# Norm weights as a scale per channel, tiles turned into shared PSUM banks, and small buffers for the gate weights

## The chip, the cores and the metric

The kernel runs on one NeuronCore of a Trainium2 chip. The metric is device time in microseconds (us) of one execution, the median of several. TensorE (PE) multiplies matrices and writes PSUM, ScalarE (ACT) evaluates functions with a scale, VectorE (DVE) does elementwise work, and SyncE (SP) issues nearly all DMA transfers between DRAM and SBUF. Each engine works its own instructions off in order and waits on semaphores for the others.

## What is computed

One layer of a hybrid block on 16 meta tokens and 512 tokens of width 1024, batch 1. Only its start matters here:

```python
h = jnp.concatenate([meta, x], axis=1)                  # 528 tokens x 1024
xn = rms_norm(h, norm_mix_g[l])                         # x / rms(x) * g, per token, g per channel
z = xn @ w_in[l]                                        # 1024 x 10752
u_rnn, u_gate, q, k, v, g_ret, ga, gb = jnp.split(z, IN_SPLITS, axis=-1)
xr = causal_dwconv(u_rnn, rnn_conv_w[l], rnn_conv_b[l])     # 4 taps over time, u_rnn is 1280 wide
hr = rg_lru(xr, rg_a_w[l], rg_a_b[l], rg_x_w[l], rg_x_b[l], lru_lambda[l])
```

Then come a retention branch of four heads, two gated projections, a residual, a second norm, a convolved feed-forward part and a last norm.

## The kernel before

Every product of f32 values runs on TensorE as three f16 products: each operand is split into a high f16 part (ACT writes it, a scaled copy) and a low f16 part (DVE: scaled operand minus the high part), and hi*hi, hi*lo and lo*hi are summed in PSUM. The helper `split` (L90 to L92) issues both instructions. Here tile names stand for `xh`, `xl`, the high and low parts of the normed input, stored with channels on partitions (8 groups k of 128 channels) and tokens along the free axis, and `wt`, the split weights.

The input is 4 tiles of 128 tokens (`xin`, two tiles to a buffer) and 16 meta tokens (`xmeta`, stored as 128 rows of 128 channels). Per tile, `rms_scale` takes the sum of squares (ACT L320), its root (ACT L322) and a reciprocal (DVE L324). `first_rows` (L403) multiplies the tile by the token's factor and by `gmix`, the norm's weights copied to all 128 partitions. `first_transpose` turns it with eight TensorE transposes into two PSUM banks, and `finish` splits each bank of 128 x 512 into `xh` and `xl`.

The recurrent branch has ten output chunks of 128 columns (n = 0 to 9). A product of one chunk has two halves of 267 token columns, each 24 f16 matmuls (8 groups k, 3 terms). The first halves of n = 0, 1, 2 need tiles 0 and 1 only and are issued early (`first_half`, L383 in the profile), between the transposes of tiles 2 and 3; their second halves follow in `conv_product`. After each product `conv_taps` (L538 on ACT, L540 on DVE) sums the four taps, and `rnn_gates` (n - 3) runs the gate products. `keep_warm` issues matmuls on zeros, so that TensorE has something to do while the input is loaded; they write the first bank of the PSUM tile that chunk 0's product later uses (`early[0]`).

PSUM has three `acc` tiles of two banks and two single banks. The order of instructions on PE, ACT and DVE is the order of the code (`manual_schedule`). Weights come in units: `unit_load` fetches one into one of two f32 buffers (`raw`), `steps` holds its splits, `tick` issues the next split, `get` issues what a product needs. Loads on SyncE's queue keep the order in which the code issues them (`load`, L93 to L102), except a few early ones that do not depend on it (the decay table `dec_meta`, L690, and two gathers `hs` of meta tokens with 1024 elements of 4 bytes each, L1068).

Of the kernel before, what the change touches and what calls it, by code (L numbers as in the profile page):

```python
# [14 lines left out]
P = 128  # L15
T = 528
# [34 lines left out]
def hybrid_block_kernel(ctx, tc, x, meta, norm_mix_g, w_in, conv_w, conv_b, rg_a_w, rg_a_b,  # L51
# [159 lines left out]

    def fast_steps(rv, bk, bc):
# [88 lines left out]
    gmix = wsp.tile([P, D], F32, name="gmix", tag="wt")  # L301
# [53 lines left out]
    xn_t = {}  # L355
# [43 lines left out]
    def first_rows(i, rs):  # L399
        xn_t[i] = pair("xn")  # L400
        for a in range(2):
            sl = slice(a * 512, (a + 1) * 512)
            nc.vector.scalar_tensor_tensor(xn_t[i][a], token_rows(i)[:, sl], rs, gmix[:, sl], op0=ALU.mult, op1=ALU.mult)  # L403

    def first_transpose(i, banks):
        xn = xn_t.pop(i)
        c0 = 3 + NM + P * i
        pvs = []
        for a in range(2):
            pv = banks[a].rearrange("p (b c) -> p b c", c=P)  # L410
            for k in range(4):
                nc.tensor.transpose(pv[:, k], xn[a][:, k * P:(k + 1) * P], ident)
            pvs.append(pv)

        def finish(*half):
            for a in half:
                sl = slice(4 * a, 4 * a + 4)
                split(xh[:, sl, c0:c0 + P], xl[:, sl, c0:c0 + P], pvs[a], S_XN)
        return finish
# [14 lines left out]
    keep_warm(18)  # L434
    pmeta = acc("pmeta")[:, 0]
    xm, gm = xmeta[:, 0:P], xmeta[0:8, P:2 * P]
    first_rows(0, rms_scale(token_rows(0), P, "n"))
    finish0 = first_transpose(0, ptr_banks())
    first_rows(1, rms_scale(token_rows(1), P, "n"))
    ssm = small.tile([P, 4], F32, name="ssm")  # L440
    nc.scalar.activation(xmeta[:, 2 * P:3 * P], xm, AF.Square, accum_out=ssm[:, 0:1])
    nc.tensor.matmul(pmeta[:, 0:P], pick[0:8, 0:P], gm, start=True, stop=True)
    nc.tensor.matmul(pmeta[:, 2 * P:2 * P + 1], same[:, 0:P], ssm[:, 0:1], start=True, stop=True)
    finish0(0)
    finish0(1)
    keep_warm(2)
    pt1 = acc("pt1")
    finish1 = first_transpose(1, [pt1[:, 0], pt1[:, 1]])
    nc.scalar.activation(ssm[:, 1:2], pmeta[:, 2 * P:2 * P + 1], AF.Sqrt, scale=1.0 / D, bias=eps_t)
    nc.vector.reciprocal(ssm[:, 2:3], ssm[:, 1:2])  # L450
    nc.vector.scalar_tensor_tensor(xm, xm, ssm[:, 2:3], pmeta[:, 0:P], op0=ALU.mult, op1=ALU.mult)
    keep_warm(5)
    nc.tensor.transpose(pmeta[:, P:2 * P], xm, ident)
    keep_warm(6)
# [3 lines left out]

    first_step()
# [4 lines left out]
    first_rows(2, rms_scale(token_rows(2), P, "n"))  # L464
    first_half(0)
    for i in range(2):
        first_step()
    finish2 = first_transpose(2, ptr_banks())
    rs3 = rms_scale(token_rows(3), P, "n")
    finish2(0, 1)  # L470
    first_rows(3, rs3)
    first_half(1)
    queue(unit_load(2))
    for i in range(4):
        first_step()
    finish3 = first_transpose(3, ptr_banks())
    first_half(2)
    finish3(0, 1)
# [34 lines left out]
    def load_gates(nm):  # L513
        src = {"a": rg_a_w, "x": rg_x_w}[nm]
        raw = wraw.tile([P, 2048], F32, name="raw")
        load(raw[:, :DR].rearrange("p (n j) -> p n j", n=NR), src.rearrange("n i j -> i n j"))
        gw[nm] = ([piece([P, 2, 512], F16, "gw") for _ in range(3)], raw)

    def split_gates(nm):
        wt, raw = gw[nm]  # L520
        for i, n in enumerate((512, 512, 256)):
            split(wt[i][:, 0, :n], wt[i][:, 1, :n], raw[:, 512 * i:512 * i + n], SW)
# [56 lines left out]
    load_gates("x")  # L579
    for n in range(NR):  # L580
# [109 lines left out]
    nc.sync.dma_start(dec_meta, decay_t[:, :, T:].rearrange("h p c -> p h c"))  # L690
# [713 lines left out]
```

## Time and profile before

| What | Value |
|---|---|
| median of 3 runs | 1076.57 us (1076.39 to 1077.71) |
| profiled execution, its own time | 1076.25 us |
| its span in the trace | 1074.5 us |
| PE busy | 1055.9 us, 98% of the span |
| DVE busy, ACT busy | 839.0 us (78%), 567.5 us (53%) |
| DMA | 112.00 MB, mean 104 GB/s |

The span is the time between the first and the last event in the trace; the execution's own time is 1.75 us longer than it. "PEclk" is the TensorE clock that was granted: the page shows it at nine tenths or more in all 40 slices. The page puts an engine's idle time down to what released it, so a row with "[1.69 <-DVE xn L403]" says that the engine had been idle 1.69 us and that the xn instruction of line 403 on DVE ended it. A row of several instructions ("x18") gives the time from the start of the first to the end of the last.

### The profile page before, as it was taken

The numbers are of one execution on the slowest core, as the hardware profiler recorded it, in microseconds if no ns is written. First come the engines' busy times: TensorE is split into PE (matmuls) and PEld (weight loads), VectorE is DVE, ScalarE is ACT, GpSimd is POOL, SyncE is SP. The second block draws the span as 40 slices with busy tenths as digits, with TensorE's granted clock in tenths as the row PEclk, the third lists the DMA queues.
The fourth block names the chain that finished last, engine by engine and source line by source line (L and its number), as shares of the span: only waits on it lengthen the run. The fifth ranks groups of instructions, "written<-read, shape, count | busy, mean of one in ns | idle before, by whom it ended". The sixth has DMA issues, their size and how long they took to land.

```text
span 1074.5 us, 20950 instructions
## 1 busy us (share of the span) xinstructions
PE 1055.9 (98%) x9037; PEld 855.1 (80%) x9037; DVE 839.0 (78%) x1219; ACT 567.5 (53%) x847; POOL 6.8 (1%) x20
## 2 busy tenths in 40 slices
PE   8999999999999999999999999999999999999997
PEld 5888888865684858888888885588888888888885
DVE  6875799998786969878697785578767777888875
ACT  6558954435564747566454453365444544454442
POOL 2000000000000000000000000000000000000000
PEclk9999999999999999999999999999999999999999
DMA  7432243431212212423333355143232323113322
GB/s 220 133 117 80 80 138 119 157 120 40 80 41 72 88 62 65 128 89 119 103 104 119 118 200 174 38 159 118 79 118 80 119 79 118 41 60 126 111 79 79
DMA packets 108027, 112.00 MB, mean 104 GB/s; under 512 B 5546, under 2 KB 99472, under 8 KB 107936
## 3 DMA queue, kind: packets, MB, share of 16 engines
q1 hardware_dynamic: 107504, 110.27, 31.4%
q8 instruction: 70, 1.15, 0.4%
q10 hardware_dynamic: 144, 0.26, 0.1%
q0 software_dynamic: 288, 0.14, 0.1%
q14 instruction: 21, 0.17, 0.0%
HBM read 108.57 MB, written 2.10 MB: 103 GB/s over the span
## 4 chain that ended last, share of the span: by engine, by line
PE 75%; DVE 14%; ACT 8%; issue 2%; DMA 1%; SPq 0%; ACTq 0%; DVEq 0%
PE ps L370 33%; PE P L1240 9%; PE pa L776 9%; PE ps L839 4%; PE pm L370 4%; PE ps L1112 4%; PE pe L776 4%; DVE wt L92 3%; PE ps L383 3%; PE pb L776 2%; ACT wt L91 2%; PE ps L861 1%; DVE rnn L575 1%; DVE raw L231 1%; ACT L627 1%
## 5 line engine op out<-in xcount | busy, mean ns | idle before, releaser
L370 PEld LDWEIGHTS <-wt 128*128 128x128 f16 x4224 | 410.5, 97 | 63.7 <-DVE t L667 1.4
L92 DVE SCALAR_TENSOR_TENSOR wt<-raw,wt 128x1024 f16<-128x1024 f32 (+2 forms) x270 | 296.6, 1111 | 71.5 <-ACT wt L91 69.5
L91 ACT ACTIVATE wt<-raw 128x1024 f16<-128x1024 f32 (+2 forms) x270 | 256.4, 965 | 161.1 <-PE ps L370 28.3
L776 PEld LDWEIGHTS <-wt 128*128 128x128 f16 x2016 | 195.0, 97 | 36.0 <-issue 8.8
L370 PE MATMUL ps<-x2h,wt 128*128 128x258 f16 x1440 | 218.8, 273 | 0.0
L370 PE MATMUL ps<-xh,wt 128*128 128x257 f16 (+2 forms) x1056 | 163.8, 275 | 1.1 <-DVE t L667 1.1
L370 PE MATMUL ps<-x2l,wt 128*128 128x258 f16 x720 | 137.7, 272 | 0.0
L1197 DVE SCALAR_TENSOR_TENSOR cv<-ps,vt,cv 128x512 f32<-128x512 f32 x96 | 71.9, 749 | 54.7 <-ACT cv L1195 53.4
L370 PE MATMUL ps<-xl,wt 128*128 128x257 f16 (+2 forms) x528 | 102.2, 275 | 0.0
L1240 PE MATMUL P<-wt,act 128*128 128x256 f16 x792 | 88.3, 273 | 0.0
L1240 PEld LDWEIGHTS <-act 128*128 128x128 f16 x792 | 77.5, 98 | 9.0
L839 PE MATMUL ps<-wt,xh 128*128 128x512 f16 x256 | 76.4, 379 | 1.2 <-DVE v L92 1.0
L776 PE MATMUL pa<-xs,wt 128*128 128x257 f16 x576 | 71.6, 273 | 4.8 <-ACT kept L781 4.5
L1195 ACT ACTIVATE cv<-ps,vt,vt 128x512 f32<-128x512 f32 x48 | 37.1, 773 | 56.8 <-PE ps L370 52.2
L370 PE MATMUL pm<-oa,wt 128*128 128x257 f16 x480 | 55.4, 274 | 0.0
L839 PEld LDWEIGHTS <-xh 128*128 128x128 f16 x256 | 24.8, 98 | 30.9 <-issue 2.9
L839 PE MATMUL ps<-wt,xl 128*128 128x512 f16 x128 | 48.5, 379 | 0.0
L776 PE MATMUL pa<-ob,wt 128*128 128x257 f16 x384 | 45.7, 274 | 0.6 <-ACT last L781 0.5
L1112 PE MATMUL ps<-wt,mx 128*128 128x512 f16 x192 | 44.3, 379 | 0.0
L231 DVE TENSOR_TENSOR raw<-raw 128x1024 f32<-128x1024 f32 x35 | 42.7, 1220 | 0.6
L1112 PEld LDWEIGHTS <-mx 128*128 128x128 f16 x192 | 17.6, 98 | 18.5
L861 PE MATMUL ps<-sc,v 128*128 128x257 f16 (+4 forms) x384 | 32.1, 236 | 0.0
(250 smaller groups left out, 1273.5 us busy)
## 6 DMA issues: line engine op xcount, KB each, us to landing
raw<-in_w_in SPq DMA_DIRECT2D x41, 1024.0 KB, 4.8
raw<-in_w_up SPq DMA_DIRECT2D x24, 1024.0 KB, 5.0
raw<-in_w_down SPq DMA_DIRECT2D x48, 256.0 KB, 3.4
raw<-in_w_branch_ret SPq DMA_DIRECT2D x16, 512.0 KB, 4.3
raw<-in_w_branch_rnn SPq DMA_DIRECT2D x8, 640.0 KB, 4.2
raw<-in_w_out SPq DMA_DIRECT2D x4, 1024.0 KB, 4.9
xin<-in_x SPq DMA_DIRECT2D x4, 512.0 KB, 4.9
h<-in_x SPq DMA_DIRECT2D x4, 512.0 KB, 4.3
```

Of the source, the lines that this page charges most:

```text
L91: nc.scalar.activation(hi, src, AF.Copy, scale=s)
L92: nc.vector.scalar_tensor_tensor(lo, src, s, hi, op0=ALU.mult, op1=ALU.subtract)
L231: nc.vector.tensor_tensor(pair, pair, rv[:, :, right].rearrange("p (h k) c -> p h k c", h=2), op=ALU.add)
L370: nc.tensor.matmul(ps[:, hf, :n], w(aw, k, col, P), src(ax, k, c0, n), start=k == 0 and (aw, ax) == (0, 0), stop=k == nk - 1 and aw == 1)
L383: mm = nc.tensor.matmul(ps[:, hf, :n], w(aw, k, col, P), src(ax, k, c0, n), start=k == 0 and (aw, ax) == (0, 0), stop=k == KD - 1 and aw == 1)
L776: nc.tensor.matmul(ps[:, :257], ws[k // 4](wf, aw, k % 4), src(xf_, ax, k), start=first and k == 0 and (aw, ax) == (0, 0), stop=k == last_ ...
L839: nc.tensor.matmul(pb, xf(ax, k, XF + j0, nb), w(aw, k % 4, 0, 512), start=i == 0, stop=i == 23)
L861: nc.tensor.matmul(ps[:, hf, s0 - lo_i:257], vt[b][:, va, d * P:(d + 1) * P], st[SCP[b][0]][:, sa, o:o + hi_i - s0], start=i == 0, stop=i ...
L1112: nc.tensor.matmul(ps[:, n], mx[k][:, a, c0:c0 + P], wo[k // 2](aw, k % 2, n * 512, 512), start=k == 0 and (a, aw) == (0, 0), stop=k == ks ...
L1195: nc.scalar.activation(vv_, ps[:, :, 2:258], AF.Identity, scale=vt2[:, 96 + ch:97 + ch], bias=b_ff[:, ch:ch + 1])
L1197: nc.vector.scalar_tensor_tensor(vv_, ps[:, :, j:j + 256], vt2[:, 48 * j + ch:48 * j + ch + 1], vv_, op0=ALU.mult, op1=ALU.add)
L1240: nc.tensor.matmul(pd[:, 256 * tt:256 * tt + 256], t[:, ax, c0 + tt * P:c0 + tt * P + P], w(wf, aw, i), start=q % 6 == 0 and tt == 0 and i ...
```

## The change

The weights of the first norm are no longer multiplied in before the transposes. They are brought to one column per channel group (`gs`, 128 x 8, by a small transpose of the 8 x 128 weights), and are the scale operand of the split: because a channel is a partition after the transpose, the scale differs from group to group, and each split of 128 x 512 becomes four of 128 x 128 (`high`, `low`). The buffer `gmix` and its load go.

For tiles 0 and 1 the token's factor goes into a diagonal matrix `dg` (identity times factor, L429), and TensorE turns and scales at once by multiplying the f32 tile with it (L452). For tiles 2 and 3 a `tensor_scalar` multiplies by the factor (L437), followed by the transposes as before (L450). Tile 1's second half, and tile 3, are turned into the second, still unused banks of `early[0]` and `early[1]`; tiles 2 and 3 are turned together, ahead of the third early product.

The first two weight chunks are one unit of 256 columns, fetched and split by columns in two pieces. The gate weights are loaded into six pieces of 128 x 512 and not into the two `raw` buffers, and are split at other places. `dec_meta` is loaded in order with the rest, and one `hs` gather then stands first on SyncE's queue, the second one behind the first two input tiles. The number of `keep_warm` matmuls changes from 18, 2, 5 and 6 to 11, 4 and 5.

```diff
-    for n in range(2):
-        u_ur.append((unit(8, P, [(0, 0, kmaj(w_in, 0, 8, o_ur + P * n, P))]), 0))
-    for i in range(1, 5):
+    for i in range(5):
         u = unit(8, 256, [(0, 0, kmaj(w_in, 0, 8, o_ur + 256 * i, 256))])
...
+    def column_unit():
...
+        def fetch(c):
+            load(rv[:, :, c * P:c * P + P], ap[:, :, c * P:c * P + P])
+        def step(i, c):
...
+                split(tv[0], tv[1], rv[:, 4 * i:4 * i + 4, c * P:c * P + P], SW)
+        queue([step(i, c) for c in range(2) for i in range(2)])
...
+    nc.scalar.dma_start(xmeta[0:8, P:2 * P], norm_mix_g.rearrange("(c f) -> c f", f=P))
     load(xin[0][:, 0], x2[0:P])
     load(xin[0][:, 1], x2[P:2 * P])
-    load(gmix, norm_mix_g.partition_broadcast(P))
     load(xmeta[:, 0:P], meta.rearrange("t (c f) -> (t c) f", f=P))
-    load(xmeta[0:8, P:2 * P], norm_mix_g.rearrange("(c f) -> c f", f=P))
-    queue(unit_load())
+    fetch = column_unit()
+    fetch(0)
     load(xin[1][:, 0], x2[2 * P:3 * P])
-    queue(unit_load())
+    fetch(1)
     load(xin[1][:, 1], x2[3 * P:4 * P])
+    fetch = column_unit()
+    fetch(0)
+    fetch(1)
...
+    def first_scale(i):
+        rs = rms_scale(token_rows(i), P, "n")
+        dg = piece([P, 512], F32, "dg")[:, 0:P]
+        nc.vector.tensor_scalar_mul(dg, ident, rs)
+        return dg
...
+        def turn(a):
             for k in range(4):
+                c = 512 * a + k * P
+                if dg is None:
+                    nc.tensor.transpose(pvs[a][:, k], xn[a][:, k * P:k * P + P], ident)
+                else:
+                    nc.tensor.matmul(pvs[a][:, k], token_rows(i)[:, c:c + P], dg, start=True, stop=True)
+        def high(a):
+            for k in range(4):
+                g = gs[:, 4 * a + k:4 * a + k + 1]
+                nc.scalar.activation(xh[:, 4 * a + k, c0:c0 + P], pvs[a][:, k], AF.Copy, scale=g)
+        def low(a):
+            for k in range(4):
+                g = gs[:, 4 * a + k:4 * a + k + 1]
+                nc.vector.scalar_tensor_tensor(xl[:, 4 * a + k, c0:c0 + P], pvs[a][:, k], g,
+                                               xh[:, 4 * a + k, c0:c0 + P], op0=ALU.mult, op1=ALU.subtract)
...
+    keep_warm(11)
...
+    dg0 = first_scale(0)
+    turn0, high0, low0 = first_transpose(0, ptr_banks(), dg=dg0)
+    nc.tensor.transpose(pmeta[:, 3 * P:3 * P + 8], gm, ident[0:8, 0:8])
+    nc.vector.tensor_scalar_mul(gs, pmeta[:, 3 * P:3 * P + 8], S_XN)
+    turn0(0)
+    turn0(1)
+    dg1 = first_scale(1)
+    pt1 = acc("pt1")
+    turn1, high1, low1 = first_transpose(1, [pt1[:, 0], early[0][:, 1]], dg=dg1)
+    high0(0)
+    nc.scalar.activation(xmeta[:, 2 * P:3 * P], xm, AF.Square, accum_out=ssm[:, 0:1])
+    high0(1)
...
+    turn1(0)
...
+    turn1(1)
+    nc.scalar.activation(ssm[:, 1:2], pmeta[:, 2 * P:2 * P + 1], AF.Sqrt, scale=1.0 / D, bias=eps_t)
+    low0(0)
+    low0(1)
+    nc.vector.reciprocal(ssm[:, 2:3], ssm[:, 1:2])
+    nc.vector.scalar_tensor_tensor(xm, xm, ssm[:, 2:3], pmeta[:, 0:P], op0=ALU.mult, op1=ALU.mult)
+    keep_warm(4)
+    nc.tensor.transpose(pmeta[:, P:2 * P], xm, ident)
+    keep_warm(5)
     first_step()
-    finish1(0)
+    high1(0)
     split(xh[:, :, 3:3 + NM], xl[:, :, 3:3 + NM], pmeta[:, P:2 * P].rearrange("p (t c) -> p c t", c=8), S_XN)
+    low1(0)
     first_step()
-    finish1(1)
...
+    high1(1)
+    low1(1)
     first_half(0)
...
+    xn2 = first_rows(2)
+    xn3 = first_rows(3)
     first_half(1)
+    turn2, high2, low2 = first_transpose(2, ptr_banks(), xn=xn2)
+    turn3, high3, low3 = first_transpose(3, [early[i][:, 1] for i in range(2)], xn=xn3)
...
     first_half(2)
...
+        raw = [piece([P, 512], F32, "graw") for _ in range(3)]
...
-            tick(2 if n in (6, 8) else 1)
+            tick(2 if n in (4, 6, 8) else 1)
```

On TensorE, where the last `keep_warm` matmul and the first f16 product meet (before: `ps_125` is the tile `early[0]`):

```order
L427 MATMUL ps_125<-warm_123 128x512
L383 LDWEIGHTS wt_213 [waits Activation_49]
L383 MATMUL ps_125<-xh_95,wt_213 128x267 [waits Activation_49]
L383 LDWEIGHTS wt_213
L383 MATMUL ps_125<-xl_96,wt_213 128x267 [waits DVE_49]
```

The same place in the changed kernel, where `early[0]` is `ps_126`, L452 turns tile 1's second half, L510 turns the meta rows, L473 is `keep_warm` and L406 the product:

```order
L452 MATMUL ps_126<-dg_170,xin0_109 128x128 x4
L473 LDWEIGHTS warm_124
L473 MATMUL ps_126<-warm_124 128x512
...
L510 MATMUL pmeta_140<-ident_86,xmeta_99 128x128 [waits DVE_49,Activation_49]
...
L473 MATMUL ps_126<-warm_124 128x512
L406 LDWEIGHTS wt_213 [waits DVE_49,Activation_49]
L406 MATMUL ps_126<-xh_95,wt_213 128x267 [waits Activation_49]
L406 LDWEIGHTS wt_213
L406 MATMUL ps_126<-xl_96,wt_213 128x267
```

Tile 1's second half, the `keep_warm` matmuls and the product now use one PSUM tile, and the wait for DVE has moved from the product's second matmul to its first weight load.

On ACT, the splits between tile 0's and the first product, before (L441 and L449 are the meta rows' square sum and root):

```order
L441 ACTIVATE xmeta_100,ssm_179<-xmeta_100 128x128 [waits DMAHW6_49]
L91 ACTIVATE xh_95<-ptr_158 128x4x128 [waits PE_49]
L91 ACTIVATE xh_95<-ptr_159 128x4x128 [waits PE_49]
L449 ACTIVATE ssm_179<-pmeta_146,eps_t_82 128x1 [waits PE_49]
L91 ACTIVATE wt_213<-raw_117 128x512 [waits DMAHW0_49]
L91 ACTIVATE xh_95<-pt1_189 128x4x128 [waits PE_49]
L91 ACTIVATE xh_95<-pmeta_146 128x8x16 [waits PE_49]
L91 ACTIVATE wt_220<-raw_117 128x512
L91 ACTIVATE xh_95<-pt1_189 128x4x128 [waits DVE_49]
```

The same stretch in the changed kernel (L457 is `high`, L498 and L504 the meta rows' square sum and root):

```order
L457 ACTIVATE xh_95<-ptr_151,gs_123 128x128 [waits DVE_49,PE_49]
L457 ACTIVATE xh_95<-ptr_151,gs_123 128x128 x3
L498 ACTIVATE xmeta_99,ssm_141<-xmeta_99 128x128 [waits DMAHW5_49]
L457 ACTIVATE xh_95<-ptr_152,gs_123 128x128 [waits PE_49]
L457 ACTIVATE xh_95<-ptr_152,gs_123 128x128 x3
L504 ACTIVATE ssm_141<-pmeta_140,eps_t_82 128x1 [waits PE_49]
L91 ACTIVATE wt_213<-raw_115 128x4x128 [waits DMAHW6_49]
L457 ACTIVATE xh_95<-pt1_172,gs_123 128x128 x4
L91 ACTIVATE xh_95<-pmeta_140 128x8x16 [waits PE_49]
L91 ACTIVATE wt_226<-raw_115 128x4x128
L457 ACTIVATE xh_95<-ps_126,gs_123 128x128 [waits PE_49]
L457 ACTIVATE xh_95<-ps_126,gs_123 128x128 x3
```

Four splits of 512 columns have become sixteen of 128, and the last group reads `ps_126`, the tile that `keep_warm` writes: its wait for PE counts up to the last of those matmuls.

On TensorE, the end of the third early half and the start of chunk 0's second half, before:

```order
L383 MATMUL ps_338<-xh_95,wt_323 128x267
L494 MATMUL ptv_378<-ident_86,v1_367 128x128 [waits DMASW3_49,DMASW2_49,DMASW4_49,DMASW1_49,DMASW5_49,DMASW0_49,DVE_49]
L495 MATMUL ptv_378<-ident_86,v2_368 128x128 [waits DMASW6_49]
L496 MATMUL ptv_378<-ident_86,v2_368 128x24 [waits DMASW7_49,DMASW0_49]
L383 LDWEIGHTS wt_213
L383 MATMUL ps_125<-xh_95,wt_213 128x267 [waits Activation_49]
```

And in the changed kernel:

```order
L406 MATMUL ps_336<-xh_95,wt_333 128x267
L557 MATMUL ptv_408<-ident_86,v1_397 128x128 [waits DMASW3_49,DMASW2_49,DMASW4_49,DMASW1_49,DMASW5_49,DMASW0_49,DVE_49]
L558 MATMUL ptv_408<-ident_86,v2_398 128x128 [waits DMASW6_49]
L559 MATMUL ptv_408<-ident_86,v2_398 128x24 [waits DMASW7_49,DMASW0_49]
L406 LDWEIGHTS wt_213 [waits DVE_49]
L406 MATMUL ps_126<-xh_95,wt_213 128x267 [waits Activation_49]
```

The new wait for DVE on the weight load counts up to the low part of tile 3's first half, which is read from the bank that this product writes.

## Rows read from the trace of the kernel before

**Rows 1.** The page, part 1: busy time, share of the span, instructions of each engine.

```profile
PE 1055.9 (98%) x9037; PEld 855.1 (80%) x9037; DVE 839.0 (78%) x1219; ACT 567.5 (53%) x847; POOL 6.8 (1%) x20
```

**Rows 2.** Windows; columns: length, busy us (instructions) of each engine, PEclk, DMA.

```profile
14.40:25.70 11.30, 11.16 (x93) 8.94 (x92) 10.55 (x21) 9.87 (x20) 0.00 (x0) 1.00 0.63 208
25.70:82.00 56.30, 56.30 (x491) 47.65 (x491) 45.68 (x62) 32.36 (x45) 0.00 (x0) 1.00 0.38 124
```

**Rows 3.** Chain that ended last; columns: start us, length us, what.

```profile
11.18 0.87 PE pt L412 x8
...
18.67 2.75 PE ps L383 x24
...
25.71 8.37 PE ps L383 x72
```

**Rows 4.** Timeline of PE; columns: start us, length us, what, [idle before].

```profile
1.51 5.57 PE L427 MATMUL ps<-warm 128*128 128x512 f16 x18 [1.51 <-DVE warm L422]
8.77 1.23 PE L412 MATMUL ptr<-ident,xn 128*128 128x128 f32 x8 [1.69 <-DVE xn L403]
9.93 0.48 PE L442 MATMUL pmeta<-xmeta,pick 8*128 8x128 f32 x2
...
13.07 1.46 PE L427 MATMUL ps<-warm 128*128 128x512 f16 x6
14.37 0.28 PE L383 MATMUL ps<-xh,wt 128*128 128x267 f16 x1
```

**Rows 5.** Timeline of SyncE's queue: the first DMA issues.

```profile
0.81 0.42 SPq L690 DMA_DIRECT2D dec_meta<-decay  x1
...
2.78 1.23 SPq L1068 DMA_DIRECT2D hs<-in_meta_tokens  x2
```

**Rows 6.** DMA packets of 1.9 to 2.5 us (decay table).

```profile
DMA packets 529, 0.05 MB, mean 88 GB/s; under 512 B 524, under 2 KB 524, under 8 KB 529
```

**Rows 7.** DMA packets of 7 to 8 us (the 4-byte gathers).

```profile
DMA packets 2024, 0.03 MB, mean 28 GB/s; under 512 B 2018, under 2 KB 2020, under 8 KB 2024
```

**Rows 8.** Timeline of ACT, columns as for PE.

```profile
5.13 1.06 ACT L320 ACTIVATE junk<-xin 128x1024 f16<-128x1024 f32 x1 [2.83 <-DMA xin<-in_x]
...
9.32 0.31 ACT L441 ACTIVATE xmeta<-xmeta 128x128 f32<-128x128 f32 x1 [1.35 <-DMA xmeta<-in_meta_tokens]
...
9.63 1.06 ACT L91 ACTIVATE xh<-ptr 128x512 f16<-128x512 f32 x2
...
12.31 0.63 ACT L91 ACTIVATE wt<-raw 128x512 f16<-128x512 f32 x1 [1.28 <-DMA raw<-in_w_in]
...
13.32 0.27 ACT L91 ACTIVATE xh<-pmeta 128x128 f16<-128x128 f32 x1
13.48 0.63 ACT L91 ACTIVATE wt<-raw 128x512 f16<-128x512 f32 x1
```

**Rows 9.** Timeline of DVE, columns as for PE.

```profile
6.64 0.16 DVE L324 RECIPROCAL rs<-sd 128x1 f32<-128x1 f32 x1 [5.19 <-ACT sd L322]
7.87 1.41 DVE L403 SCALAR_TENSOR_TENSOR xn<-xin,rs,gmix 128x512 f32<-128x512 f32 x2 [1.07 <-DMA gmix<-in_norm_mix_g]
...
12.17 0.35 DVE L451 SCALAR_TENSOR_TENSOR xmeta<-xmeta,ssm,pmeta 128x128 f32<-128x128 f32 x1
...
14.18 0.28 DVE L92 SCALAR_TENSOR_TENSOR xl<-pmeta,xh 128x128 f16<-128x128 f32 x1
14.38 0.68 DVE L92 SCALAR_TENSOR_TENSOR wt<-raw,wt 128x512 f16<-128x512 f32 x1
```

**Rows 10.** ACT by form, 25 to 130 us; columns: xcount, busy us, mean ns, idle.

```profile
L562 ACT ACTIVATE rnn<-rnn,cpos 128x528 f32<-128x528 f32 x10 | 6.5, 727 | 0.0
L91 ACT ACTIVATE xs<-rnn 128x528 f16<-128x528 f32 x10 | 6.4, 640 | 18.0 <-DVE rnn L540 18.0
```

**Rows 11.** DVE by form, 0 to 30 us, same columns.

```profile
L498 DVE TENSOR_SCALAR vt<-ptv 128x144 f32<-128x144 f32 x1 | 0.3, 297 | 0.0
```

**Rows 12.** Timeline of PE at a product of f32 operands.

```profile
296.06 1.11 PE L876 MATMUL ps<-ssum,ones 128*128 128x257 f32 x4 [0.22 <-DVE ssum L869]
```

More of the change, by code (lines that the diff above doesn't have):

```diff
@@ L210, in unit_load, with run @@
         return [step(i, c) for i in range(2) for c in range(cuts)]
+    def column_unit():
+        _, ncol, parts, _ = units[len(loaded)]
+        raw = wraw.tile([P, 2048], F32, name="raw")
+        rv = raw.rearrange("p (k c) -> p k c", c=ncol)
+        ap = parts[0][2]
+        tiles = []
+        def fetch(c):
+            load(rv[:, :, c * P:c * P + P], ap[:, :, c * P:c * P + P])
+        def step(i, c):
+            def run():
+                if c == 0:
+                    tiles.append(wsp.tile([P, 2, 1024], F16, name="wt"))
+                tv = [tiles[i][:, a].rearrange("p (k c) -> p k c", c=ncol)[:, :, c * P:c * P + P] for a in range(2)]
+                split(tv[0], tv[1], rv[:, 4 * i:4 * i + 4, c * P:c * P + P], SW)
+            return run
+        loaded.append(len(loaded))
+        wviews.append(lambda a, k, c0, m: tiles[k // 4][:, a, k % 4 * ncol + c0:k % 4 * ncol + c0 + m])
+        queue([step(i, c) for c in range(2) for i in range(2)])
+        return fetch
     def fast_steps(rv, bk, bc):
@@ L397, in token_rows, with first_rows, first_transpose @@
         return xin[i // 2][:, i % 2]
-    def first_rows(i, rs):
-        xn_t[i] = pair("xn")
+    gs = const.tile([P, KD], F32, name="gs")
+    def first_scale(i):
[3 more added lines that the diff above has]
+        return dg
+    def first_rows(i):
+        rs = rms_scale(token_rows(i), P, "n")
+        xn = pair("xn")
         for a in range(2):
[L402 to L406, printed above, removed]
+            nc.vector.tensor_scalar_mul(xn[a], token_rows(i)[:, 512 * a:512 * a + 512], rs)
+        return xn
+    def first_transpose(i, banks, dg=None, xn=None):
         c0 = 3 + NM + P * i
-        pvs = []
-        for a in range(2):
-            pv = banks[a].rearrange("p (b c) -> p b c", c=P)
+        pvs = [b.rearrange("p (b c) -> p b c", c=P) for b in banks]
+        def turn(a):
             for k in range(4):
[L412 to L419, printed above, removed]
+                c = 512 * a + k * P
[12 more added lines that the diff above has]
+                                               xh[:, 4 * a + k, c0:c0 + P], op0=ALU.mult, op1=ALU.subtract)
+        return turn, high, low
     warm = work.tile([P, 512], F16, name="warm", tag="w")
@@ L432, in ptr_banks @@
         return [bank("ptr") for _ in range(2)]
[L434 to L454, printed above, removed]
     def first_step():
@@ L468, in hybrid_block_kernel @@
[L468 to L471, printed above, removed]
-    first_half(1)
[L473 to L476, printed above, removed]
-    first_half(2)
-    finish3(0, 1)
+    first_step()
+    first_step()
+    xn2 = first_rows(2)
+    xn3 = first_rows(3)
+    first_half(1)
+    turn2, high2, low2 = first_transpose(2, ptr_banks(), xn=xn2)
+    turn3, high3, low3 = first_transpose(3, [early[i][:, 1] for i in range(2)], xn=xn3)
@@ L481, in hybrid_block_kernel @@
+    for a in range(2):
+        turn2(a)
+    for a in range(2):
+        turn3(a)
+    first_step()
+    first_step()
+    first_half(2)
+    for a in range(2):
+        high2(a)
+        low2(a)
+    for a in range(2):
+        high3(a)
+        low3(a)
+    first_step()
+    first_step()
     v1 = work.tile([P, T], F32, name="v1", tag="w")
@@ L513, in load_gates @@
     def load_gates(nm):
-        src = {"a": rg_a_w, "x": rg_x_w}[nm]
-        raw = wraw.tile([P, 2048], F32, name="raw")
-        load(raw[:, :DR].rearrange("p (n j) -> p n j", n=NR), src.rearrange("n i j -> i n j"))
+        src = {"a": rg_a_w, "x": rg_x_w}[nm].rearrange("n i j -> i n j")
+        raw = [piece([P, 512], F32, "graw") for _ in range(3)]
+        for i, n in enumerate((4, 4, 2)):
+            load(raw[i][:, :n * P].rearrange("p (n j) -> p n j", n=n), src[:, 4 * i:4 * i + n])
         gw[nm] = ([piece([P, 2, 512], F16, "gw") for _ in range(3)], raw)
@@ L521, in split_gates @@
         for i, n in enumerate((512, 512, 256)):
-            split(wt[i][:, 0, :n], wt[i][:, 1, :n], raw[:, 512 * i:512 * i + n], SW)
+            split(wt[i][:, 0, :n], wt[i][:, 1, :n], raw[i][:, :n], SW)
     xr_split = {}
@@ L579, in hybrid_block_kernel @@
     load_gates("x")
+    queue(unit_load())
     for n in range(NR):
```

21 lines of the change are left out of this document (11 added, 10 removed).

## The prediction

> **What bounds the kernel now.** I read the page's share of busy time first: PE is busy for 1055.9 us of 1074.5 [rows 1], so only some 18 us are there to be won at all. The table of windows says where they are not: from 25.70 to 82.00 PE is busy 56.30 of 56.30 us, and from 14.40 to 25.70 it is busy 11.16 of 11.30 [rows 2]. The chain of waits agrees, since from the first product on it runs along PE through that whole stretch [rows 3]. The reader is to see that in this stretch nothing but PE's own work counts: whatever brings its first f16 product forward or puts it back goes through to the end, and what the change does to ACT or DVE after 26 us is hidden unless it makes PE wait. The change also drops some warm-up matmuls, but those stand ahead of the first product and fill waiting time. So there are three questions: when does the first f16 product start (14.37 now [rows 4]), how long is it from there to chunk 0's second half (25.71 [rows 3]), and does PE meet a new wait behind that.
>
> Why the start is 14.37 is read from the timelines of PE, ACT and DVE [rows 4, 8, 9]. Tile 0 is there at 5.13. DVE has its factor at 6.80 and then stands still 1.07 us for `gmix`; its multiplication begins at 7.87, and the transposes at 8.77, after PE's warm-up has run out at 7.08 (1.69 us idle). ACT then waits 1.28 us for the first weights, until 12.31. The last thing ahead of the product is a row of short splits on ACT and DVE, with the warm-up of 13.07 beside it.
>
> **First part: the new head, up to the first product.** Removed: the wait for `gmix` and two `xn` multiplications a tile (1.41 us a pair). Added: one `tensor_scalar` of 128 x 128 for `dg`, at most .30 us by the nearest row, 128 x 144 in .297 [rows 11]. So `dg` of tile 0 is there at 6.80 + .30 = 7.1, and the turning begins there and not at 8.77: 1.65 us gained.
>
> The turning is now a true f32 product. Four f32 instructions of 257 columns end 1.11 us after the first has begun, tail included [rows 12], which makes about .215 between starts with a tail of .45; a product of 128 columns by two instructions is half as long each, so .22. Eight transposes took .87 [rows 3], the eight products take 1.76: .9 more a tile. The first bank is ready at 7.1 + .88 + tail = 8.35, the second at 9.2. The bounds are .11 (a transpose) and .43 (below, third rival).
>
> The splits come next, where the change costs most. A split of 128 x 512 becomes four of 128 x 128. On ACT a piece of 128 x 128 lasts .27, and the next begins .16 behind it (13.32, 13.48 [rows 8]). The scale now is a column of numbers, and the one row pair that has both shows .727 against .640 at 128 x 528 [rows 10], so .09 more. A piece starts .25 behind the one before, and four last 3 x .25 + .36 = 1.11; two whole splits took 1.06 together [rows 8], that is .53 each. On DVE the piece of 128 x 128 starts .20 ahead of the next (14.18, 14.38), and an instruction that takes a column as scale lasts .35 against .28 [rows 9], so .267 a piece and 1.15 for four, against .68. Each group of four low parts waits for all four high parts.
>
> Now the sum, with these. ACT: first group 8.37 to 9.49, the meta rows' square .19, second group to 10.80, the root .2, the first weight split to 11.40, third group to 12.52, the meta rows' split .25 and the second weight split .52 to 13.76. DVE: low parts of the first two groups end at 11.97 (the second waits for ACT's 10.80), reciprocal .16, the meta rows' multiplication .35 [rows 9], which ends at 12.48. PE turns the meta rows at 12.6 and then runs five warm-up matmuls, six of which last 1.46 [rows 4]; they are through at 13.98. Here is the new wait: tile 1's second bank and the warm-up share a PSUM tile, so ACT's fourth group may not begin before 13.98, though its data have been there since about 11. It runs 14.02 to 15.14. Its four low parts wait for it and end at 16.31. The first product's weight load waits for the last of them: 16.45, against 14.37. That is **+2.08**. What is queued behind ACT's waiting piece is only what comes later (the next weight splits, the squares of tiles 2 and 3), and DVE behind it has nothing to do for PE before 19.2.
>
> By the Trainium skill, "Perfetto Trace Analysis", section "Optimizing Scalar/DVE Operations", every ACT and DVE instruction carries a fixed access overhead, and larger operations pay it less often; the rows agree in direction, .53 for one piece of 512 against 1.11 for four of 128. The Trainium skill, "ScalarE: Activation LUTs", section "What ACT_TABLE_LOAD costs", gives 186 ns + .833 ns a column, 93 ns for a pointer operand and 93 ns of overlap, an estimate of .293 a piece where the rows give .25; the sum by it would be some .9 us more, about 1079.3.
>
> **What covers the loads.** The first weights were waited for until 12.31; they are needed at 10.9 now, and stand behind fewer bytes, since `gmix` (512 KB) has gone. I cost them at nothing; if the cover fails, ACT's later wait for 13.98 still hides up to .2 us, and beyond that each us late is one on the third and fourth groups. The gate weights no longer wait for a raw buffer; ACT has slack before it needs them, so nothing gained or lost. On SyncE's queue one gather of 1024 four-byte elements now stands ahead of tile 0, in place of the decay table. Issuing: two in 1.23 against .42 for one [rows 5], so .2 more. Packets: 2018 in under a us [rows 7] makes .43 for 1024, the table's some 520 took .6 [rows 6]; at that rate 1024 take 1.2. So tile 0 is between .0 and .8 later; near the rows of the gather itself I take **+.2**.
>
> **Second part: from the first product to chunk 0's second half.** It took 25.71 - 14.37 = 11.3. In it are three halves of 2.75 and nineteen transposes at .11 [rows 3], three of them for small vectors: 8.25 + 2.1, with a handover 10.4. The .9 left are waits at tile 2's and tile 3's transposes. These now run in one go, and their `xn` come from a `tensor_scalar` and stand ready about 20.2, when PE gets there at 21.95: **-.9**. Between nothing and this is the range.
>
> **Third part: chunk 0's second half.** Its first weight load now waits for the low parts of tile 3's first half. The first bank is turned at 22.7; ACT has that group at 23.85, then three groups of low parts run in turn on DVE, 1.07 + 1.07 + 1.15, to 27.14. PE gets there at 16.45 + 10.4 = 26.83: **+.3**, zero to 1 us. The splits of chunk 4's weights now come behind chunk 2's taps, and not before: its last low part (.68 for 512 columns [rows 9]) may be late for PE; I take **+.15**, between nothing and .7. Behind that the order on PE is the old one.
>
> **Sum:** 2.08 + .2 - .9 + .3 + .15 = +1.83. The profiled execution took 1076.25, .32 below the median of 1076.57; the sum is against its trace and goes onto the median: 1076.57 + 1.83 = 1078.4 us.
>
> **Rivals.**
> - *Small pieces cost more on ACT* (slower). Three groups of four on ACT lie on the path to the first product, two ahead of the meta rows and one behind the warm-up; above .267 a piece ACT also sets the pace of the groups behind the third half. At .36 a piece (scale column fully serial) this is 12 x .11 + about .9: 1080.6. For it: only one pair of rows shows the scale's price, at 528 columns in SBUF. Against it: the starts at 13.32 and 13.48. It decides from .27 a piece.
> - *The clock falls* in PE's new gap of 2.5 us, 13.98 to 16.45 (slower). Before, it was idle 1.69 us [rows 4] and the granted clock afterwards was 1.00 [rows 2], 2.4 GHz. At half the clock the first products would lose some 1.5 us: 1080. A longer gap is not shown. The Trainium skill, "TensorE: Matmul & The Clock Gate", section "What's actually happening", makes the granted clock hang on what PE did shortly before; this gap is a case of it, and the row of 1.69 us alone does not bear it out.
> - *The f32 products take .43* (slower). The only f32 product of 128 columns, L442, has two instructions in .48, tail included, that start .21 apart [rows 4]; were that the pace for all sixteen, tile 1's turning and the warm-up behind it end 2.6 us later: 1081. Against it are four of twice the columns at the same pace [rows 12].
> - *The column scale costs nothing* and the gather neither: pieces at .16 and .20. Then the warm-up ends at 12.5, the first product starts at about 14.2, and the gain of .9 stays: 1075.6.
>
> **How the numbers follow.** Two tenths of a per cent, 2.15 us, is about what a measurement of this kernel can tell from no change: same is 1074.4 to 1078.7. Forecast .50 (its own spread, 1077.4 to 1079.2: .37 same, .13 slower); small pieces .17 (slower but for .02); clock .06; f32 products .08; costless scale .19 (.06 faster, .13 same, for the later wins may add). Together faster .06, same .52, slower .42. The range goes from the costless scale to the dear pieces, 1075.6 to 1080.6; the f32 rival and a larger gain are left out.
>
> **What would show it.** In the profile after: turning starts at about 7.2; ACT's pieces about .25 apart; PE idle about 2.5 us ahead of the first product, released by DVE's low part, with the warm-up over by 14; the first product at 16.6; tiles 2 and 3 turned in one stretch of 1.75 us; a wait of some .3 at chunk 0's second half; granted clock 1.00 throughout. I am wrong if the first product starts before 15.5, if the four ACT pieces are done in under .9, if PE's gap shows ACT or a DMA as releaser, or if PE waits again between 30 and 82 us.

## The result: 3.6 us slower, and what the profile after shows

| Kernel | Median | Executions | Ratio to before, 95% interval |
|---|---|---|---|
| before | 1076.62 us | 8 (1076.36 to 1078.19) | |
| changed | 1080.21 us | 8 (1078.41 to 1081.40) | 1.003 [1.0019, 1.0041] |
| changed, measured again (e11) | 1079.73 us | 5 (1079.55 to 1081.53) | 1.0035 [1.0021, 1.0049] |

The time is inside the range of the prediction (1075.6 to 1080.6), 1.8 us above its centre (1078.4). The executions do not lie around their median: of the first eight spans one is 1076.3, five are 1077.5 to 1078.3, two are 1079.4 and 1079.5. Each execution's mean granted clock of TensorE was taken too: .999 for the one at 1076.3, .997 for the five, .996 and .995 for the two. The first is what the sum gave. The means of the others are lower, and a fall of the clock was among the rivals; a second delay (below, e11) was in no text.

A part of the 3.6 us lies outside the span. In all 87 executions of the kernel before that were measured beside the experiments the time exceeds the span by 1.66 to 1.92 us; in the first eight of the changed kernel it does so by 1.73 to 2.66, 2.0 at the median. That makes some .3 us, which no trace shows; its cause stays open.

The timeline of PE in the profiled execution of the changed kernel (span 1077.7; columns as in [rows 4]) shows the head:

```profile
7.44 2.05 PE L452 MATMUL ptr<-dg,xin 128*128 128x128 f32 x16 [1.02 <-DVE dg L429]
...
12.90 0.30 PE L510 MATMUL pmeta<-ident,xmeta 128*128 128x128 f32 x1
13.04 1.24 PE L473 MATMUL ps<-warm 128*128 128x512 f16 x5
...
16.77 0.38 PE L406 MATMUL ps<-xh,wt 128*128 128x267 f16 x1 [2.48 <-DVE xl L462]
16.94 0.43 PE L406 MATMUL ps<-xl,wt 128*128 128x267 f16 x1
17.16 0.65 PE L406 MATMUL ps<-xh,wt 128*128 128x267 f16 x2
```

The reader is to see three things: the first tile is turned 1.3 us earlier than before (7.44 against 8.77 [rows 4]), the first product begins 2.4 us later (16.77 against 14.37), and ahead of it PE is idle for 2.48 us, which a low part on DVE ends. The lengths say a fourth thing: after the first matmul at 16.77 the next begin at 16.94 and 17.16, and those behind about .22 apart, where the same matmul of 267 columns took .115 in the kernel before (24 in 2.75 [rows 3]).

ACT and DVE in the same execution (two views, same columns):

```profile
8.63 1.14 ACT L457 ACTIVATE xh<-ptr,gs 128x128 f16<-128x128 f32 x4 [0.47 <-PE ptr L452]
...
13.24 0.28 ACT L91 ACTIVATE xh<-pmeta 128x128 f16<-128x128 f32 x1 [0.29 <-PE pmeta L510]
13.42 0.62 ACT L91 ACTIVATE wt<-raw 128x512 f16<-128x512 f32 x1
14.32 1.14 ACT L457 ACTIVATE xh<-ps,gs 128x128 f16<-128x128 f32 x4 [0.28 <-PE ps L473]
```

```profile
7.09 0.29 DVE L429 TENSOR_SCALAR dg<-ident,rs 128x128 f32<-128x128 f32 x1
...
13.77 1.12 DVE L462 SCALAR_TENSOR_TENSOR xl<-pt,gs,xh 128x128 f16<-128x128 f32 x4
14.80 0.68 DVE L92 SCALAR_TENSOR_TENSOR wt<-raw,wt 128x512 f16<-128x512 f32 x1
15.49 1.12 DVE L462 SCALAR_TENSOR_TENSOR xl<-ps,gs,xh 128x128 f16<-128x128 f32 x4
```

Four pieces take 1.14 on ACT and 1.12 on DVE (two whole splits took 1.06 on ACT [rows 8], one .68 on DVE [rows 9]). ACT's last group starts at 14.32, and what ended its wait is L473, the warm-up: the shared PSUM tile does what the order of the instructions said.

Windows of the changed kernel; columns: length, busy us of PE, PEld, DVE, ACT and POOL (instructions), PEclk, DMA share, GB/s:

```profile
14.40:17.00 2.60, 0.23 (x2) 0.19 (x3) 2.58 (x8) 2.60 (x7) 0.00 (x0) 0.86 1.16 285
17.00:20.00 3.00, 3.00 (x17) 2.06 (x16) 2.57 (x8) 2.94 (x8) 0.00 (x0) 0.56 1.20 290
20.00:25.70 5.70, 5.70 (x53) 5.12 (x51) 1.76 (x4) 1.66 (x7) 0.00 (x0) 1.00 0.97 278
```

PE is busy for all of 17 to 20 us and gets 17 matmuls done, with a granted clock of .56; [rows 2] had 1.00 there. A matmul of 267 columns in .222 us, about twice the .115, is the lower level, 1.2 GHz. Narrower windows, same columns, show when the clock fell:

```profile
15.50:16.00 0.50, 0.00 (x0) 0.00 (x0) 0.50 (x2) 0.50 (x2) 0.00 (x0) 1.00 1.18 292
16.00:16.50 0.50, 0.00 (x0) 0.00 (x0) 0.50 (x3) 0.50 (x2) 0.00 (x0) 0.75 1.16 291
16.50:17.00 0.50, 0.23 (x2) 0.19 (x3) 0.50 (x2) 0.50 (x1) 0.00 (x0) 0.50 1.17 290
```

It fell inside the idle gap, ahead of the first product. The chain of waits gives the bill (start us, length us, what):

```profile
16.77 7.06 PE ps L406 x48
23.83 0.87 PE ptr L450 x8
24.70 0.87 PE ps L450 x8
25.58 2.75 PE ps L406 x24
...
28.73 8.44 PE ps L406 x72
37.16 67.79 PE ps L393 x594
```

Two halves take 7.06; at full clock the same 48 matmuls took 5.67 (e2 and e11, below). The sixteen transposes run without a break. Chunk 0's second half begins at 28.73. In the kernel before, the chain's 25.71 [rows 3] counts from the end of the transpose ahead of it, and PE's timeline has that product's start at

```profile
25.64 0.29 PE L383 MATMUL ps<-xh,wt 128*128 128x267 f16 x1
```

so it is 3.1 us later now. The long run behind it is without a wait, and the span is 3.2 us longer.

### The profile page after: what moved, and what is told of

Read it like the earlier page. It is cut to its first block, busy times and chain, and to the rows that moved or that the text cites. A ratio compares the mean times of both kernels' runs of the same rounds, so it can differ in the third digit from the quotient of the medians.

```text
span 1077.7 us, 21019 instructions
## 1 busy us (share of the span) xinstructions
PE 1057.3 (98%) x9043; PEld 856.9 (80%) x9043; DVE 839.3 (78%) x1242; ACT 570.7 (53%) x871; POOL 6.9 (1%) x20
## 3 DMA queue, kind: packets, MB, share of 16 engines
q8 instruction: 70, 1.15, 0.5%
## 4 chain that ended last, share of the span: by engine, by line
PE 77%; DVE 14%; ACT 6%; issue 2%; DMA 0%; SPq 0%; ACTq 0%; DVEq 0%
PE ps L393 35%; PE P L1306 9%; PE pa L842 9%; PE ps L905 4%; PE pm L393 4%; PE ps L1178 4%; PE pe L842 4%; DVE wt L92 3%; PE ps L406 3%; PE pb L842 2%; ACT wt L91 2%; PE ps L927 1%; DVE rnn L639 1%; DVE raw L253 1%; DVE v L92 1%
## 5 line engine op out<-in xcount | busy, mean ns | idle before, releaser
L393 PEld LDWEIGHTS <-wt 128*128 128x128 f16 x4224 | 410.5, 97 | 63.7 <-DVE t L733 1.4
L842 PEld LDWEIGHTS <-wt 128*128 128x128 f16 x2016 | 195.0, 97 | 36.0 <-issue 8.8
L406 PEld LDWEIGHTS <-wt 128*128 128x128 f16 x288 | 28.5, 100 | 8.0 <-ACT wt L91 2.9
```

The lines of the kernel that those rows point to most:

```text
L393: nc.tensor.matmul(ps[:, hf, :n], w(aw, k, col, P), src(ax, k, c0, n), start=k == 0 and (aw, ax) == (0, 0), stop=k == nk - 1 and aw == 1)
L406: mm = nc.tensor.matmul(ps[:, hf, :n], w(aw, k, col, P), src(ax, k, c0, n), start=k == 0 and (aw, ax) == (0, 0), stop=k == KD - 1 and aw == 1)
L842: nc.tensor.matmul(ps[:, :257], ws[k // 4](wf, aw, k % 4), src(xf_, ax, k), start=first and k == 0 and (aw, ax) == (0, 0), stop=k == last_ ...
```

## The experiments

Theory W: the shared tile and the small pieces put the first product back, the idle time that this leaves lets TensorE's clock fall, and the joint transposes give some .9 back. Rival X: the early products are slow for another reason, such as the loads beside them, whose share of the DMA engines is higher than before in that stretch (1.16 to 1.20).

| Run | Median (executions) | Before, same chip | Ratio, 95% interval | Spans |
|---|---|---|---|---|
| e1_own_bank | 1076.75 (11) | 1076.33 | 1.0006 [.9997, 1.0015] | 1074.3 to 1076.1 |
| e2_fill_gap | 1078.29 (11) | 1076.33 | 1.0022 [1.0013, 1.0031] | 1076.3 to 1078.4 |
| e3_whole_splits | 1077.68 (11) | 1076.33 | 1.0013 [1.0004, 1.0022] | 1075.0 to 1076.6 |
| e4_before_gap | 1076.63 (11) | 1076.33 | 1.0002 [.9993, 1.0011] | 1074.3 to 1075.8 |
| e5_head_warm | 1076.56 (11) | 1076.21 | 1.0003 [.9994, 1.0012] | 1074.3 to 1075.6 |
| e6_single_bank | 1075.95 (11) | 1076.21 | .9996 [.9987, 1.0005] | 1073.6 to 1075.1 |
| e7_table_first | 1076.48 (11) | 1076.21 | 1.0002 [.9993, 1.0011] | 1074.1 to 1076.0 |
| e8_before_turns | 1076.28 (11) | 1076.21 | .9998 [.9989, 1.0006] | 1074.1 to 1074.9 |
| e9_bank_warm | 1075.81 (11) | 1076.39 | .9995 [.9986, 1.0003] | 1073.9 to 1075.4 |
| e10_before_gates | 1076.52 (11) | 1076.39 | 1.0000 [.9991, 1.0009] | 1074.4 to 1074.9 |
| e11_after_again | 1079.73 (5) | 1076.39 | 1.0035 [1.0021, 1.0049] | 1077.6 to 1079.1 |

**e1_own_bank.** Does the shared tile hold the product back?

```diff
-    turn1, high1, low1 = first_transpose(1, [pt1[:, 0], early[0][:, 1]], dg=dg1)
+    turn1, high1, low1 = first_transpose(1, [pt1[:, 0], pt1[:, 1]], dg=dg1)
```

> Edit: tile 1's second half is turned into the second bank of the tile that holds its first half (as in the kernel before), so that it no longer shares a PSUM tile with the warm-up and the first product. Theory W (the shared tile holds the first product back, and the gap that this leaves lets TensorE's clock fall): the first product begins at about 14.1 and goes on as pieces come, its half ends at about 17.4 (17.3 in the kernel before, 20.3 in the changed one), the granted clock stays at 1.00, and the time is about 1076 us, 4 us under the changed kernel's 1080.2. Rival X (the slow early products have another cause, such as the loads that run beside them): the start is the same, but the early products stay slow, 1077.5. If the shared tile is not what holds the product: 1080.

One word changed, and of the 3.6 us over the kernel before .4 are left. The first product begins at 14.18, right behind the last warm-up matmul. It stops once, since ACT's last group now waits for DVE, which reads the other half of the same tile. ACT's timeline and the chain of this run:

```profile
14.98 1.14 ACT L457 ACTIVATE xh<-pt,gs 128x128 f16<-128x128 f32 x4 [0.88 <-DVE xl L462]
```

```profile
16.56 4.18 PE ps L406 x35
...
22.48 2.75 PE ps L406 x24
...
25.64 8.44 PE ps L406 x72
```

The halves are through at 20.74 (the first at about 17.8, expected at 17.4), and chunk 0's second half begins at 25.64, as in the kernel before. In this profile the granted clock was 1.00 from 12 to 600 us; four of the eleven spans lie at 1075.6 to 1076.1, two of them with a mean clock of .997. The DMA share in 14.4 to 20 was 1.17 to 1.19, no less than in the changed kernel, and the matmuls were at full speed: that speaks against X. It does not part the late start from the clock; the next run does.

**e2_fill_gap.** Is the idle time the cause of the slow matmuls?

```diff
     keep_warm(5)
+    wb = bank("wb")
+    for _ in range(11):
+        nc.tensor.matmul(wb, warm[:, 0:P], warm, start=True, stop=True)
```

> Edit: eleven more warm-up matmuls, into a bank of their own, between the last warm-up matmul and the first product, so that PE is busy in the gap of 14.3 to 16.7; nothing else changes. Theory W: the first product still begins at about 16.8, the two early halves take 5.5 us and not 7.06, the granted clock is 1.00 throughout, time 1078.6 with little spread. Rival X (loads or PSUM beside the products slow them): the two halves still take 7 us, 1080.2.

Its windows:

```profile
14.40:17.00 2.60, 2.49 (x13) 1.00 (x11) 2.58 (x9) 2.53 (x7) 0.00 (x0) 1.00 1.16 286
17.00:20.00 3.00, 3.00 (x27) 2.54 (x27) 2.57 (x7) 2.94 (x8) 0.00 (x0) 1.00 1.20 290
```

```profile
16.92 5.67 PE ps L406 x48
```

The product begins no earlier (16.92), the loads are the same (1.16 and 1.20), but 27 matmuls are done between 17 and 20 and not 17, at a clock of 1.00. Work that computes nothing takes the difference to the kernel before from 3.6 to 2.0 us. X falls, also because in the changed kernel the clock fell ahead of the first product, and because e11 (below) has matmuls at full speed beside the same loads. Seven of eleven spans are 1076.3 to 1076.5, as the one lowest of the changed kernel. Ten of the eleven have a mean clock of .998 or .999; in the changed kernel, e11 included, ten of thirteen have .997 or less. The spread was not as small as expected: four spans are 1077.5 to 1078.4, three of them at .999, so what they lost they lost elsewhere.

**e3_whole_splits.** What do the small pieces cost? (This kernel leaves the norm's weights out.)

```diff
-            for k in range(4):
-                g = gs[:, 4 * a + k:4 * a + k + 1]
-                nc.scalar.activation(xh[:, 4 * a + k, c0:c0 + P], pvs[a][:, k], AF.Copy, scale=g)
+            nc.scalar.activation(xh[:, 4 * a:4 * a + 4, c0:c0 + P], pvs[a], AF.Copy, scale=S_XN)
...
```

> Edit: the splits of the four tiles are whole again, 128 x 512 with one constant scale; the norm's weights are left out of the normed tokens. Theory W: ACT's last group takes .55 and not 1.14, DVE's .68 and not 1.12, so the first product begins at about 15.6; the gap is 1.35 us, the clock stays at 1.00, and the time is about 1077.4: 1.2 from the pieces and 1.6 from the clock. Rival X: only the 1.2, 1079.0.

PE's timeline has the start where it was expected:

```profile
15.57 0.27 PE L406 MATMUL ps<-xh,wt 128*128 128x267 f16 x1 [1.42 <-DVE xl L458]
```

That is 1.2 us earlier than in the changed kernel, with a gap of 1.42 in which the clock of this execution stayed at 1.00. So the pieces make 1.2 us of the late start; the other 1.2 stay with whole splits, behind the warm-up that the shared tile waits for. The span of this execution is 1075.0. Five of the eleven are 1076.5 or 1076.6, three of these with a mean clock of .997: the clock probably fell in some of them, which no trace shows.

**e4_before_gap.** Does idle time at this place cost the kernel before anything?

```diff
-    keep_warm(5)
     nc.tensor.transpose(pmeta[:, P:2 * P], xm, ident)
-    keep_warm(6)
```

> Edit, in the kernel before: the last eleven warm-up matmuls (five and six) are left out, so that PE is idle from about 12.0 to 14.4 but for one transpose. Theory W: the clock falls there too, the first early halves take some 1.5 us more, 1078.1. Rival X (a gap of this length does nothing): 1076.6, unchanged.

Windows and chain of this run:

```profile
14.40:17.00 2.60, 2.60 (x16) 1.81 (x15) 1.93 (x5) 2.57 (x7) 0.00 (x0) 0.58 0.86 316
17.00:20.00 3.00, 3.00 (x23) 2.49 (x22) 2.10 (x5) 2.19 (x6) 0.00 (x0) 0.79 0.70 246
```

```profile
14.23 4.46 PE ps L383 x23
...
19.56 2.75 PE ps L383 x24
...
26.33 8.37 PE ps L383 x72
```

The clock fell as expected (.58), and the first half took 4.46 for 23 matmuls. The idle time was not one gap: PE waited .62 us ahead of the transpose, .49 ahead of the first matmul (13.36) and .59 ahead of the second (14.23), and the clock fell after these three. But the time hardly moved: chunk 0's second half begins .62 later in this execution, and the median is not clear of no change. My 1.5 was too much, because in the kernel before the eight transposes of tile 2 and those of tile 3 take 1.36 and 1.14 us with their waits and .87 without, and a slow first half uses these .8 us up. In the changed kernel this slack is gone, so there the whole loss counts. The size failed, the mechanism held.

**e5_head_warm and e7_table_first** changed e1 by one thing each: 16 warm-up matmuls at the head and not 11, and the decay table first on SyncE's queue.

> Edit: as e1_own_bank, and the first block of warm-up matmuls is 16 and not 11, so that PE is busy until about 7.3, when the first tile is turned, and not only until 6.3. The executions of e1_own_bank lie in two groups, spans of about 1074.5 and 1076.0. Theory H (in the slower executions the clock falls in the gap of 6.3 to 7.4 at the head): the upper group goes, spans of 1074.5, median 1076.4. Rival (the upper group has another cause, such as a late load): two groups as before, median about 1076.8.

> Edit: as e1_own_bank, and the decay table is issued as in the kernel before, so that it and not the gather of 1024 four-byte elements stands first on SyncE's queue. If the gather costs what the sum says (.2 us), tile 0 lands at 5.13 and not at 5.30, the time is .2 lower, 1076.5, and the two groups of spans stay. If the gather also is the cause of the upper group (spans of 1076.0), that group goes.

Neither gave a clear difference. In e5 no span of 1076.0 is left and no mean clock below .998, but eleven executions are few to call that shown. In e7 three spans of 1076.0 stay, and the first tile landed at 5.25; with the gather first it landed at 5.33 (e1) and 5.28 (changed kernel); since it lands at 4.80 to 5.11 in four profiles of the kernel before and its variants, the gather is not shown to be what delays it. What does stays open.

**e8_before_turns.** The joint transposes alone, in the kernel before.

```diff
-    first_rows(2, rms_scale(token_rows(2), P, "n"))
     first_half(0)
...
+    first_rows(2, rms_scale(token_rows(2), P, "n"))
+    first_rows(3, rms_scale(token_rows(3), P, "n"))
     first_half(1)
     queue(unit_load(2))
+    finish2 = first_transpose(2, ptr_banks())
+    finish3 = first_transpose(3, [early[i][:, 1] for i in range(2)])
...
```

> Edit, in the kernel before: tiles 2 and 3 are normed after the first early half and turned together ahead of the third one, into the two single banks and the free banks of the first two products' tiles, as in the changed kernel; the norm's weights, the splits and the loads stay as they were. My theory: the .9 us of waits at the transposes between the early halves go, but the second product may wait for its weights by some .4; chunk 0's second half begins at 25.2 or before (25.7 in the kernel before), time 1075.6 to 1076.0. Rival (the gain needs the new loads and splits by columns, or the waits only move behind the third half): 1076.4, unchanged.

Unchanged, as the rival said. In the profiled execution the transposes ran in one go, and the stretch from the first product (14.96, the load of `gmix` came late here) to chunk 0's second half was 10.73 and not 11.27; but the chain ran over DVE:

```profile
23.84 1.81 DVE xl L92 x3
25.65 0.04 issue
25.69 8.42 PE ps L383 x72
```

The third low part on DVE sets the second half's start, since weight splits stand ahead of it there. That is the wait of my third part. The changed kernel has it too, and there it cost .08 (below).

**e10_before_gates.** The gate weights and ticks alone.

> Edit, in the kernel before: the recurrence's gate weights are loaded into six pieces and not into the two raw buffers, and their splits and the ticks stand where the changed kernel has them; nothing else changes. My sum: nothing, 1076.3, PE busy without a break from 26 to 82 us. Rival (their loads, beside the first products, hold up tiles or weights, or a split of weights comes late for chunk 4): a wait at chunk 3 to 5 of .2 to .7, 1076.5 to 1077.

```profile
30.00:82.00 52.00, 52.00 (x454) 44.01 (x452) 43.14 (x55) 30.75 (x44) 0.00 (x0) 1.00 0.31 102
```

PE has no gap: this part costs nothing, as the sum had it.

**e11_after_again.** The changed kernel once more.

> The changed kernel itself, on the same chip and against the same runs of the kernel before as the two others. If the lost clock is a matter of the gap of 2.9 us, its profile shows the first half at .22 us a matmul again and the spans again lie 2 to 5 us above 1074.5: 1080 for the median. If the fall of the clock was peculiar to the first measurement: 1078.4, the sum without it.

The median of the first expectation came (1079.73), its slow matmuls did not: the profile caught an execution with the same gap (2.48 us, and not the 2.9 of the expectation) and without the fall. PE's timeline and the chain:

```profile
16.69 0.28 PE L406 MATMUL ps<-xh,wt 128*128 128x267 f16 x1 [2.48 <-DVE xl L462]
```

```profile
16.69 5.67 PE ps L406 x48
...
24.11 2.75 PE ps L406 x24
27.26 8.44 PE ps L406 x72
35.69 67.79 PE ps L393 x594
```

This is the sum alone: chunk 0's second half 1.62 after the kernel before, the stretch behind it 1.61. Yet the span was 1077.6, 3.1 more than before; ACT's and PE's timelines far behind have the rest:

```profile
643.13 2.00 ACT L91 ACTIVATE wt<-raw 128x1024 f16<-128x1024 f32 x2 [5.62 <-DMA raw<-in_w_out]
```

```profile
645.46 2.82 PE L842 MATMUL pa<-ob,wt 128*128 128x257 f16 x24 [1.18 <-ACT kept L847]
```

In the changed kernel's first profile ACT's row has a wait of 3.47. One transfer of `w_out` landed late, ACT's split came late, and PE waited 1.2 us for ACT, a wait that the kernel before does not have there. Of the other four executions three have a mean clock of .997 and one, with a span of 1077.8, has .999.

**e6_single_bank and e9_bank_warm.** A version that has neither wait.

```diff
-    turn1, high1, low1 = first_transpose(1, [pt1[:, 0], early[0][:, 1]], dg=dg1)
+    turn1, high1, low1 = first_transpose(1, [pt1[:, 0], bank("pt1b")], dg=dg1)
...
-    keep_warm(4)
+    keep_warm(3)
```

> Edit, in the changed kernel: tile 1's second half is turned into a bank of its own (a single bank, which neither the warm-up nor tile 1's first half uses), and the second block of warm-up is 3 and not 4. Theory W: ACT's last group of small pieces need wait neither for the warm-up (14.3) nor for the low parts of tile 1's first half (14.9 in e1_own_bank); it runs 13.95 to 15.0, the low parts 15.5 to 16.6, the first half of chunk 0 ends at about 17.0 (17.9 in e1_own_bank, 17.3 before), so the time is some .9 us under e1_own_bank and .6 to .9 under the kernel before: 1075.6. Rival (the path runs over DVE's order and the loads): as e1_own_bank, 1076.7.

e9 is the same with 16 matmuls at the head:

> Edit: as e6_single_bank (own single bank for tile 1's second half, second warm-up block of 3), and the first warm-up block is 16 and not 11. Theory W with H: the first product begins at about 14, its half ends at about 17, no waits at the transposes, clock 1.00 at the head; chunk 0's second half begins at 24.6 (25.7 before); spans of about 1073.6 with the executions above 1075 gone but for late loads; median 1075.5, 0.7 to 0.9 us under the kernel before. Rival (the head's gain is given back at later waits, as for the 1 MB load at 634 us that landed late in e6_single_bank): 1076.2, unchanged.

The chain of e6, and ACT's row at the load of `w_out`:

```profile
14.00 1.49 PE ps L406 x13
15.51 4.18 PE ps L406 x35
...
24.59 8.44 PE ps L406 x72
```

```profile
640.27 2.00 ACT L91 ACTIVATE wt<-raw 128x1024 f16<-128x1024 f32 x2 [5.49 <-DMA raw<-in_w_out]
```

In e6 chunk 0's second half begins 1.05 us before the kernel before, and six of its spans lie at 1073.6 to 1073.9, where the lowest of 33 of the kernel before was 1074.2. The profiled one met the late load (5.49) and lost 1.05 again. In e9 that half begins at 25.22 and not at the 24.6 expected: in its profile the 16 warm-up matmuls ran to 7.6, so that PE turned the first tile at 7.79, though its factor matrix had been there since 7.26 (e6: 7.10 and 7.14). The longer fill was itself on the path there. Both medians, e6's and e9's, are below the kernel before by .26 and .58 us, but neither interval excludes 1. Ten of e9's eleven executions (1075.59 to 1076.06) lie below the lowest of the 21 of the kernel before (1076.16): the gain is likely, not shown by the intervals.

## Why the prediction was right, and where it was lucky

- **The head.** Turning from 7.1 (measured 7.44, of it .17 from a later landing), eight f32 products in 1.76 (sixteen instructions 2.05, tail included, .11 apart), four pieces in 1.11 and 1.15 (1.14, 1.12), warm-up through at 13.98 (14.28), first product at 16.45 plus .2 (16.77). Every term held to .34, and half of that is the landing, for which the sum had taken .2. That the landing came out so is luck as far as these runs go: the .2 was put down to the gather, and with the table first (e7) the tile landed as late. The loads were covered, as the sum had it: ACT's first weight split (11.30) waited for no DMA. The f32 rival is out.
- **The wait on the shared tile** was read from the order of the instructions, not from any time, and e1 showed it to be the pivot: 3.2 of the 3.6 us hang on it, directly or through the clock.
- **The joint transposes.** -.9 forecast; in e11, with the clock up, the stretch took 10.57 against 11.27, of it .08 the later wait below, so -.78.
- **The later waits** were too dear: +.3 at chunk 0's second half came out as .08 (that matmul starts .244 behind the one before it, against .169), +.15 at chunk 4 as nothing. In e11, the head, transposes and waits make +1.6, where the sum gave +1.83.
- **The clock.** Here the prediction failed in a chance. The rival's price was near (some 1.5 us, for which no working was given; 7.06 - 5.67 = 1.39), but it was given .06 on the ground that a gap of 1.69 had done nothing. A row on a shorter gap bounds nothing for a longer one: I wrote that a longer gap is not shown, and should have given the two outcomes about equal chances. One profile also bounds little for the shorter gap: seven of the 87 executions of the kernel before have a mean clock of .997 and spans of 1075.9 to 1076.5, and all others have at least .998 and at most 1075.1. Where in those seven the clock fell no trace shows. In the changed kernel ten of thirteen have .997 or less, so by these means the forecast "granted clock 1.00 throughout" was wrong more often than right.
- **Luck.** The sum gave 1078.4. The profile adds up otherwise: 1.7 for the sum's own terms (2.4 at the head, .7 given back behind it), 1.4 for the clock, 3.1 together; most of what is left of the 3.6 us is of the size of the time outside the span (.3), which was not foreseen. The range reached 1080.6 for the dear pieces, and those did not come (four in 1.14); the rival that did come was priced at 1080, so that 1080.2 lies inside by a bound drawn for something else. By the prediction's own limits the likeliest outcome, no clear change (up to 1078.7, .52), did not come, and slower (.42) did.
- **The late load** was not foreseen. It was seen in three profiles (e5, e6, e11), all of kernels that contain the change; none of the four of the kernel before and its variants shows it, nor do the six other profiles with the change. Whether the shift of the program brings it about or chance does, these runs do not settle.

## What to carry to other kernels

When scratch work such as warm-up matmuls and real data shared a PSUM tile, the reader of the real data waited for the last of the scratch work (e1: 3.2 of 3.6 us); look in the order of the instructions for which tile each wait really counts. The idle gap ahead of the dense stretch had two prices, its own length and, in most executions, the clock afterwards (1.4 us). A slack further on hid part of the second in e4; once removed, it lay bare. A gain of under 1 us in a kernel of 1076 was given back by one late transfer: compare the spans and mean clocks of the executions one by one, not the medians alone, and do not take one profile for all of them.

## What was not expected of the hardware

- The same kernel with the same gap of 2.48 us at the same place once ran about 13 matmuls at the lower clock (.222 us for 267 columns, granted clock .56) and once at the upper (.115, 1.00). The Trainium skill, "TensorE: Matmul & The Clock Gate", section "What's actually happening", lets recent activity decide; what differed between the two executions these profiles do not show. In e4 the clock fell (.58) behind three waits of only .49 to .62 us, with one instruction between each two; in its profile the kernel before had one wait of 1.69 and 1.00 behind it.
- One 1 MB load took about 2 us longer to land in three profiles of thirteen (waits of 5.42 to 5.62 on ACT and not 3.40 to 3.68). PE waited 1.0 to 1.2 us by it, 600 us behind the change.
- The first tile's landing spreads over .6 us between profiles (4.80 to 5.42), three times the .2 that the sum had taken for what stands ahead of it on the queue.
